# Two parts of the transposed activations in one 512-column product

## The chip, the cores and the metric

The kernel runs on one core of a Trainium2 chip, in one launch. The metric is the device time of the program in microseconds, as the median of several runs; less is better. The engines are TensorE (PE, with its weight loads as PEld), VectorE (DVE), ScalarE (ACT), GpSimd (POOL) and SyncE (SP), which here only issues transfers.

## The reference

An encoder trunk of two layers over 256 tokens of width 1024. Each layer normalises x, multiplies it with one wide input matrix, and feeds three branches: a chunkwise retention (8 heads), a sparse attention over a compressed latent, whose keys a small indexer chooses, and a cross-attention into 256 memory tokens. The branches are projected, gated with sigmoids, summed, projected once more and added to x. Then comes the feed-forward part, which is more than half of the weights that are read:

```python
        x = x + merged @ w_out[l]
        h2 = rmsnorm(x, norm2[l])
        x = x + jnp.square(jax.nn.relu(h2 @ w_ff1[l])) @ w_ff2[l]
```

All inputs and the output are float32.

## The kernel before

**Products in two parts.** Every large product is made of float32r operands. An operand a is split into a high part (a copy into float32r) and a low part (what is left), and `mm3` (L217) issues three products into one accumulation: high x high, low x high and high x low. In the code hi and lo are the parts of a weight block, xh and xl those of the activations.

**The weight stream.** All weights come as blocks of 128 x 1024 in the order of `plan()`. `load_next` has SP fetch a block into wst (four buffers); `split_next` (L154) makes whi on ACT (L162) and wlo on DVE (L163), five buffers each. `use` (L173) hands out the next block after `ahead` (L167) has issued the splits of the blocks up to four further on; the split of a block waits for the products that still read its buffer. The order of each engine's instructions is that of the program text.

**A-form and B-form.** `gemm_a` (L222) keeps the activations as stationary operand and streams 512 columns of weights past them: out rows are tokens. `gemm_b` (L234) does the reverse: a weight block of 128 output columns is stationary and the 256 tokens stream past, so the result comes out transposed. B-form serves mq (the queries of the memory attention, 4 blocks a layer), mk (the keys of the memory, 4 blocks a layer) and f1 (the first feed-forward matrix, 32 blocks a layer). Two blocks make a group: they fill one PSUM tile of 128 x (2 x 256), which `evac` then reads.

**The feed-forward part** (`ff`, L833). The first four f1 blocks are held together (ws, pp, `first`, L851), while the second half of the normalised x is still being transposed (`turn`, L860) and row statistics are made; `ahead` (L875, L878) issues splits between them; `spread` (L305) brings the row factor R into the columns' layout over a PSUM tile and an ACT copy (L310). Then `evac` (L838) makes relu, scale and square of each group: DVE (L840), ACT (L842), DVE (L843, L845). From i = 2 to 15 a step is one group of f1 followed by the products of f2 for group i - 2 (`second`, L884), A-form with the squares uh and ul as stationary operand.

**Layer 1's start.** `Between` (L905) and `k_evac` (L947): the last products of layer 0's feed-forward, `norm_half(0)`, then mk with `norm_half(1)` (L277; transposes into two PSUM tiles) between its two groups, since x's second half is finished only then. The evaluation of mk is `k_part` (L753).

**Buffers.** PSUM has eight banks, four under the tag mm and four under sd; a tile takes a whole bank. A tile gets the buffer of its tag that was released first. In SBUF the tag a4 has 22 buffers of 4 KB per partition, among them the parts of x and of the memory (`ht_pair`, L262: two buffers), and b2 has 10 of 2 KB. Attention work runs as lanes: generators that `tick` (L184) advances by a step after each weight block, with pauses counted in blocks.

```python
            for j in range(2):
                hi, lo = (v3(w, 8, 128) for w in use(name))
                for k in range(8):
                    xh, xl = xT[k // 4]
                    mm3(p[:, j], hi[:, k], lo[:, k], xh[:, k % 4], xl[:, k % 4], k == 0, k == 7)
```

Of the kernel before, what the change touches and what calls it, by code (L numbers as in the profile page):

```python
# [18 lines left out]
COLS = {"rq": 0, "rk": 512, "rv": 1024, "rg": 1536, "dsa": 2048, "mq": 2472, "g0": 2984, "g1": 4008, "g2": 5032}  # L19


# blocks of the weight stream that go by before the next step of a lane, in each layer
PAUSE = {
# [11 lines left out]
def plan():  # L35
    seq = []

    def a_form(name, l, src, c0, n, nk):
        for k in range(0, nk, 2):
            seq.append((name, src, l, "A", c0, n, k))  # L40

    def b_form(name, l, src, c0, n):
        for c in range(0, n, 128):
            seq.append((name, src, l, "B", c0 + c, 128, 0))

    def heads(l):
        a_form("dsa", l, "w_in", COLS["dsa"], 424, 8)
        for n in ("rq", "rk", "rv"):
            a_form(n, l, "w_in", COLS[n], 512, 8)
        a_form("iq", l, "w_iq", 0, 256, 2)  # L50
        b_form("mq", l, "w_in", COLS["mq"], 512)
        a_form("uq", l, "w_uq", 0, 512, 2)
        seq.append(("ukv", "w_uk", l, "K", 0, 512, 0))

    for l in range(L):
        if l:
            b_form("mk", l, "w_mem_kv", 0, 512)
        heads(l)
        a_form("rg", l, "w_in", COLS["rg"], 512, 8)
        if not l:  # L60
            b_form("mk", l, "w_mem_kv", 0, 512)
        a_form("mv", l, "w_mem_kv", 512, 512, 8)
        for b, o in ((0, "w_ret_o"), (2, "w_mem_o"), (1, "w_dsa_o")):
            for c in range(2):
                a_form(f"g{b}", l, "w_in", COLS[f"g{b}"] + 512 * c, 512, 8)
            for c in range(2):
                a_form(f"o{b}", l, o, 512 * c, 512, 4)
        for c in range(2):
            a_form("wo", l, "w_out", 512 * c, 512, 8)
        for i in range(18):  # L70
            if i < 16:
                b_form("f1", l, "w_ff1", 256 * i, 256)
            if i >= 2:
                for k in range(2):
                    seq.append(("f2", "w_ff2", l, "F", 0, 1024, 2 * (i - 2) + k))
    return seq
# [19 lines left out]
def trunk(ctx: ExitStack, tc: tile.TileContext, x, xt, mem, memt, wts, gains, rel_bias, final_norm,  # L96
# [8 lines left out]
    dr = ctx.enter_context(tc.tile_pool(name="dr", bufs=1, space=bass.MemoryType.DRAM))  # L105
    ctx.enter_context(tc.manual_schedule())

    NB = {"a4": 22, "b2": 10, "s1": 6, "st": 4, "w": 5}

    def a4(shape, name, dt=F32):  # L110
        return act.tile(shape, dt, name=name, tag="a4", bufs=NB["a4"])
# [25 lines left out]
    def bc(col, *shape):  # L137
        return col.unsqueeze(2).to_broadcast([128, *shape])

    # the weight stream: blocks arrive in the order of plan(), each split into two float32r parts  # L140
    SEQ = plan()
    OFF = np.concatenate([[0], np.cumsum([128 * block_cols(b) for b in SEQ])]).tolist()
    st_tiles, split_tiles = {}, {}
# [33 lines left out]
        pos["use"] = i + 1  # L177
        return split_tiles.pop(i)

    # attention and other work beside the products of the stream, a step after every block  # L180
    lanes = []
    now = [0]

# [38 lines left out]
    def gemm_a(name, xT, nk, n, pst):  # L222
        for k0 in range(0, nk, 2):
            hi, lo = (v3(w, 2, n) for w in use(name))
            for t in range(2):
                for j in range(2):
                    k = k0 + j
                    xh, xl = xT[k // 4]
                    mm3(pst[t][:, :n], xh[:, k % 4, tsl(t)], xl[:, k % 4, tsl(t)], hi[:, j], lo[:, j],
                        k == 0, k == nk - 1)  # L230
            if k0 < nk - 2:
                tick()

    def gemm_b(name, xT, ncols, evac):  # L234
        for c in range(0, ncols, 256):
            p = mm().rearrange("p (j t) -> p j t", j=2)
            for j in range(2):
                hi, lo = (v3(w, 8, 128) for w in use(name))
                for k in range(8):
                    xh, xl = xT[k // 4]  # L240
                    mm3(p[:, j], hi[:, k], lo[:, k], xh[:, k % 4], xl[:, k % 4], k == 0, k == 7)
                if j == 0:
                    tick()
            evac(c // 128, p)
            tick()

    def transpose4(p, src):
# [14 lines left out]
    def ht_pair(name):  # L262
        return a4([128, 4, 256], name + "h", F32R), a4([128, 4, 256], name + "l", F32R)

    def mem_load(c):
        tmp = a4([128, 4, 256], "gxt")
        nc.sync.dma_start(tmp, memt[:, 4 * c:4 * c + 4])
        return tmp

    def mem_gain(tmp, l, c):  # L270
        pair = ht_pair("gx")
        V.tensor_mul(tmp, tmp, bc(gn[:, 16 + 8 * l + 4 * c:20 + 8 * l + 4 * c], 4, 256))
        mT.append(pair)
        yield
        split_to(tmp, *pair)

    def norm_half(c, gcol):  # L277
        pair = ht_pair("xT")
        for t in range(2):
            p4 = transpose4(mm(), X[t][c])  # L280
            tmp = b2([128, 4, 128], "ntmp")
            V.tensor_mul(tmp, p4, bc(gn[:, gcol + 4 * c:gcol + 4 * c + 4], 4, 128))
            split_to(tmp, pair[0][:, :, tsl(t)], pair[1][:, :, tsl(t)])
        return pair
# [17 lines left out]
        yield  # L302
        row_rstd(X, "n1", r=rstd)

    def spread(r, name):  # L305
        p = mm()
        for t in range(2):
            PE.transpose(p[:, tsl(t)], r[:, t:t + 1].to_broadcast([128, 128]), ident)
        R = s1([128, 256], name)
        S.activation(R, p[:, :256], AF.Copy)  # L310
        return R

    # constants and inputs
    gn = cst.tile([128, 54], F32, name="gn")
    nc.sync.dma_start(gn, gains)
    zero = cst.tile([128, 512], mybir.dt.bfloat16, name="zero")
# [3 lines left out]
        PE.matmul(warm, zero[:, :128], zero, start=True, stop=True)  # L320
    xT0 = []
    for c in range(2):
        pair = ht_pair("gx")
        xT0.append(pair)
        tmp = a4([128, 4, 256], "gxt")
        for k in (0, 2):
            nc.sync.dma_start(tmp[:, k:k + 2], xt[:, 4 * c + k:4 * c + k + 2])
            load_next()
            (G if c + k else V).tensor_mul(tmp[:, k:k + 2], tmp[:, k:k + 2], bc(gn[:, 4 * c + k:4 * c + k + 2], 2, 256))
            split_to(tmp[:, k:k + 2], pair[0][:, k:k + 2], pair[1][:, k:k + 2])  # L330
            split_next()
# [501 lines left out]
    def ff(l, xT, side, tail):  # L833
        gcol = 32 + 8 * l
        us = {}
        R = []

        def evac(i, p):  # L838
            r = b2([128, 2, 256], "fr")
            V.scalar_tensor_tensor(r, p, 0.0, R[0][:, None, :].to_broadcast([128, 2, 256]), op0=OP.max, op1=OP.mult)  # L840
            uh = b2([128, 2, 256], "uh", F32R)
            S.activation(uh, r, AF.Square)  # L842
            V.tensor_mul(r, r, r)  # L843
            ul = b2([128, 2, 256], "ul", F32R)
            V.tensor_sub(ul, r, f(uh))  # L845
            us[i] = (uh, ul)

        ws = [[v3(w, 8, 128) for w in use("f1", n)] for n in range(4)]
        pp = [v3(mm(), 2, 256) for _ in range(2)]

        def first(i, kh, j):  # L851
            hi, lo = ws[2 * i + j]
            for k in range(4 * kh, 4 * kh + 4):
                xh, xl = xT[kh]
                mm3(pp[i][:, j], hi[:, k], lo[:, k], xh[:, k % 4], xl[:, k % 4], k == 0 and j == 0, k == 7,
                    skip_group_check=True)

        pair, tmps = ht_pair("xT"), []

        def turn(t):  # L860
            tmp = b2([128, 4, 128], "ntmp")
            V.tensor_mul(tmp, transpose4(mm(), X[t][1]), bc(gn[:, gcol + 4:gcol + 8], 4, 128))
            split_to(tmp, pair[0][:, :, tsl(t)], pair[1][:, :, tsl(t)])

        first(0, 0, 0)
        turn(0)
        first(0, 0, 1)
        turn(1)
        xT.append(pair)
        for j in range(2):  # L870
            first(1, 0, j)
        rstd = row_rstd(X, "n2")
        for j in range(2):
            first(0, 1, j)
        ahead(pos["use"] - 2)  # L875
        for j in range(2):
            first(1, 1, j)
        ahead(pos["use"])  # L878
        R.append(spread(rstd, "R"))
        evac(0, pp[0])  # L880
        evac(1, pp[1])
        acc = [[sd(), sd()], [sd(), sd()]]

        def second(i, k, hi, lo, c, t):  # L884
            uh, ul = us[i]
            mm3(acc[t][c], uh[:, k, tsl(t)], ul[:, k, tsl(t)], hi[:, c], lo[:, c], i == 0 and k == 0, i == 15 and k == 1)

        for i in range(2, 16):
            gemm_b("f1", xT, 256, lambda c, p: evac(i, p))
            for k in range(2):  # L890
                hi, lo = (v3(w, 2, 512) for w in use("f2"))
                for c in range(2):
                    for t in range(2):
                        second(i - 2, k, hi, lo, c, t)
                tick()
            if i in side:
                side[i]()
        last = [(i, k, *[v3(w, 2, 512) for w in use("f2", 2 * (i - 14) + k)]) for i in (14, 15) for k in range(2)]
        for c, t in tail.order:
            for i, k, hi, lo in last:  # L900
                second(i, k, hi, lo, c, t)
            V.tensor_add(X[t][c], acc[t][c], X[t][c])
            tail(c, t)
# [166 lines left out]
```

## Time and profile before

| | us |
|---|---|
| median of 3 runs | 887.86 |
| lowest and highest | 887.8 and 888.34 |
| span of the profiled execution, first to last instruction | 886.7 |
| TensorE busy in it | 876.5 |
| VectorE busy | 625.2 |
| ScalarE busy | 468.0 |

The profile is of one execution; of its own time only the span is known. Matmuls are pipelined and their ends in the profile are modelled, so the busy time of a group of products overstates what each adds; the distance from one start to the next does not. A wait is put down to the instruction whose semaphore came last.

### The profile page before, as it was taken

What the parts mean: (1) busy time and instruction counts of PE and PEld (TensorE: products, weight loads), DVE (VectorE), ACT (ScalarE), POOL (GpSimd) and SP (SyncE); (2) the same over time, 40 slices, a digit from 0 to 9 for tenths busy, and PEclk for the clock granted to TensorE, in tenths of its full rate; (3) what the DMA queues carried; (4) which work ended last, traced back from release to release, by engine and by line L of the source; (5) the groups of instructions that cost most, each with busy time, mean ns of one, the idle gap of its engine ahead of it and who ended that gap; (6) DMA issues with size and microseconds to landing.
All of it is one profiled execution on the core that took longest, in us unless ns stands there. A gap on an engine that the chain in (4) does not pass through costs nothing.

```text
span 886.7 us, 13129 instructions
## 1 busy us (share of the span) xinstructions
PE 876.5 (99%) x5119; PEld 767.1 (87%) x5119; DVE 625.2 (71%) x910; ACT 468.0 (53%) x673; POOL 21.7 (2%) x27
## 2 busy tenths in 40 slices
PE   8999999999999999999999999999999999999996
PEld 6888988888889999999898888888888999999995
DVE  5878788786777656666578758996858685555554
ACT  6576458575545444444256555676574544444442
POOL 2000110000000000000001001000000000000000
PEclk9999999999999999999999999999999999999999
DMA  8883345536354655665546543454545465666541
GB/s 310 291 304 126 118 167 170 209 120 200 134 194 137 217 186 182 203 210 190 162 153 225 179 157 98 163 189 145 176 157 174 162 211 190 190 190 190 182 152 48
DMA packets 45711, 158.76 MB, mean 179 GB/s; under 512 B 5160, under 2 KB 6480, under 8 KB 45520
## 3 DMA queue, kind: packets, MB, share of 16 engines
q1 hardware_dynamic: 45360, 157.40, 53.7%
q8 instruction: 40, 0.66, 0.3%
q10 hardware_dynamic: 288, 0.52, 0.2%
q14 instruction: 23, 0.19, 0.1%
HBM read 156.84 MB, written 1.06 MB: 178 GB/s over the span
## 4 chain that ended last, share of the span: by engine, by line
PE 98%; issue 1%; DVE 0%; DMA 0%; ACT 0%; POOLq 0%; POOL 0%; SPq 0%; DVEq 0%
PE mm L218 22%; PE mm L220 21%; PE mm L219 21%; PE sd L220 9%; PE sd L218 9%; PE sd L219 9%; PE mm L249 1%; PE sd L567 1%; PE sd L655 1%; PE sd L249 1%; PE sd L596 1%; PE sd L520 1%; PE sd L640 0%; PE sd L624 0%; PE sd L497 0%
## 5 line engine op out<-in xcount | busy, mean ns | idle before, releaser
L163 DVE TENSOR_TENSOR wlo<-wst,whi 128x1024 fp32r<-128x1024 f32 (+1 forms) x286 | 342.7, 1216 | 144.9 <-ACT whi L162 143.5
L162 ACT ACTIVATE whi<-wst 128x1024 fp32r<-128x1024 f32 (+1 forms) x286 | 297.1, 1050 | 181.6 <-PE mm L220 56.4
L218 PE MATMUL mm<-xTh,whi 128*128 128x256 f32 x544 | 154.4, 284 | 0.0
L220 PE MATMUL mm<-xTl,whi 128*128 128x256 f32 x544 | 153.8, 283 | 0.0
L219 PE MATMUL mm<-xTh,wlo 128*128 128x256 f32 x544 | 153.7, 283 | 0.0
L219 PEld LDWEIGHTS mm<-xTh,wlo 128*128 128x128 f32 x544 | 104.1, 191 | 1.3
L218 PEld LDWEIGHTS mm<-xTh,whi 128*128 128x128 f32 x544 | 104.0, 191 | 1.2
L220 PEld LDWEIGHTS mm<-xTl,whi 128*128 128x128 f32 x544 | 104.1, 191 | 0.0
L220 PE MATMUL sd<-wlo,uh 128*128 128x512 f32 x256 | 101.1, 395 | 0.0
L218 PE MATMUL sd<-whi,uh 128*128 128x512 f32 x256 | 101.0, 395 | 0.0
L219 PE MATMUL sd<-whi,ul 128*128 128x512 f32 x256 | 100.9, 394 | 0.0
L218 PE MATMUL mm<-whi,gxh 128*128 128x512 f32 (+1 forms) x208 | 82.0, 394 | 1.2 <-ACT whi L162 1.2
L220 PE MATMUL mm<-wlo,gxh 128*128 128x512 f32 (+1 forms) x208 | 81.3, 391 | 1.1 <-DVE wlo L163 1.1
L219 PE MATMUL mm<-whi,gxl 128*128 128x512 f32 (+1 forms) x208 | 81.2, 390 | 0.0
L218 PE MATMUL mm<-whi,xTh 128*128 128x512 f32 (+1 forms) x176 | 68.8, 391 | 0.0
L220 PE MATMUL mm<-wlo,xTh 128*128 128x512 f32 (+1 forms) x176 | 68.1, 387 | 0.0
L219 PE MATMUL mm<-whi,xTl 128*128 128x512 f32 (+1 forms) x176 | 68.1, 387 | 0.0
L842 ACT ACTIVATE uh<-fr 128x512 fp32r<-128x512 f32 x32 | 20.2, 632 | 77.1 <-DVE fr L840 77.1
L220 PEld LDWEIGHTS sd<-wlo,uh 128*128 128x128 f32 x256 | 48.2, 188 | 11.2
L218 PEld LDWEIGHTS sd<-whi,uh 128*128 128x128 f32 x256 | 48.4, 189 | 10.0
L219 PEld LDWEIGHTS sd<-whi,ul 128*128 128x128 f32 x256 | 48.3, 188 | 10.0
L218 PEld LDWEIGHTS mm<-whi,gxh 128*128 128x128 f32 x208 | 39.6, 191 | 9.6 <-ACT whi L162 1.8
(243 smaller groups left out, 1358.3 us busy)
## 6 DMA issues: line engine op xcount, KB each, us to landing
wst<-in_wts_dram SPq DMA_DIRECT2D x276, 512.0 KB, 3.9
wst<-in_wts_dram SPq DMA_DIRECT2D x8, 424.0 KB, 4.5
gxt<-in_memt_dram SPq DMA_DIRECT2D x4, 512.0 KB, 5.7
gxt<-in_xt_dram SPq DMA_DIRECT2D x4, 256.0 KB, 5.4
X<-in_x_dram SPq DMA_DIRECT2D x4, 256.0 KB, 5.8
decay<-in_decay_dram SPq DMA_DIRECT2D x1, 1024.0 KB, 5.4
mrow<-in_mem_dram SPq DMA_DIRECT2D x2, 512.0 KB, 5.4
Bt<-scr SPq DMA_DIRECT2D x1, 1024.0 KB, 6.9
```

What stands on the lines that cost most here:

```text
L162: S.activation(hi[:, :n], st[:, :n], AF.Copy)
L163: V.tensor_sub(lo[:, :n], st[:, :n], f(hi[:, :n]))
L218: PE.matmul(p, ah, bh, start=start, stop=False, **kw)
L219: PE.matmul(p, al, bh, start=False, stop=False, **kw)
L220: PE.matmul(p, ah, bl, start=False, stop=stop, **kw)
L249: PE.transpose(p[:, tsl(j)], src[:, tsl(j)], ident)
L520: PE.matmul(p[:, j], Q3[t][:, h + j], K3[:96], start=True, stop=True)
L567: PE.matmul(p[:, j * K:j * K + K], qd[rows, h // 2, tsl(t)], kd[rows, h // 2, :K], start=True, stop=True)
L596: PE.transpose(p[:, tsl(j)], bm[:, h0 + j - g0, tsl(s)], ident)
L655: PE.matmul(p[:, hs], sc0[h // 4][:, h % 4, tsl(t)], v[:, 0, hs], start=True, stop=t == 0)
L842: S.activation(uh, r, AF.Square)
```

## The change

The two parts of the transposed activations come to lie in one tile of a new tag, x8 (`ht_both`, four buffers of 8 KB), and a4 goes from 22 to 15 buffers. In B-form `mm2` takes the place of `mm3`: the stationary high weights meet both parts in one product of 512 columns (two runs of 256), and the low weights meet the high part in a second product of 256 columns, added to the first half. A weight block now fills a whole PSUM bank, so a group has two of them. `halves` adds the two halves at eviction: ACT copies the second half of each bank to a b2 tile, DVE adds the first half to it. The evaluations read that tile in place of PSUM. In `ff` the four held blocks take four mm banks; the transposes of `turn` and `spread` move to sd banks. `gemm_a` reads the same parts as before. The pauses of the lanes stay as they were.

```diff
@@ -105,7 +105,7 @@
     dr = ctx.enter_context(tc.tile_pool(name="dr", bufs=1, space=bass.MemoryType.DRAM))
     ctx.enter_context(tc.manual_schedule())
 
-    NB = {"a4": 22, "b2": 10, "s1": 6, "st": 4, "w": 5}
+    NB = {"a4": 15, "x8": 4, "b2": 10, "s1": 6, "st": 4, "w": 5}
 
     def a4(shape, name, dt=F32):
         return act.tile(shape, dt, name=name, tag="a4", bufs=NB["a4"])
@@ -225,23 +225,37 @@
             for t in range(2):
                 for j in range(2):
                     k = k0 + j
-                    xh, xl = xT[k // 4]
+                    xh, xl = xT[k // 4][:2]
                     mm3(pst[t][:, :n], xh[:, k % 4, tsl(t)], xl[:, k % 4, tsl(t)], hi[:, j], lo[:, j],
                         k == 0, k == nk - 1)
             if k0 < nk - 2:
                 tick()
 
+    def mm2(p, hi, lo, pair, k, start, stop):
+
+        xh, _, both = pair
+        PE.matmul(p, hi, both[:, :, k], start=start, stop=False, skip_group_check=True)
+        PE.matmul(p[:, 0], lo, xh[:, k], start=False, stop=stop, skip_group_check=True)
+
+    def halves(s, ps2):
+        for j, p in enumerate(ps2):
+            S.activation(s[:, j], p[:, 1], AF.Copy)
+            V.tensor_add(s[:, j], p[:, 0], s[:, j])
+
     def gemm_b(name, xT, ncols, evac):
         for c in range(0, ncols, 256):
-            p = mm().rearrange("p (j t) -> p j t", j=2)
+            ps2 = []
             for j in range(2):
                 hi, lo = (v3(w, 8, 128) for w in use(name))
+                p = v3(mm(), 2, 256)
+                ps2.append(p)
                 for k in range(8):
-                    xh, xl = xT[k // 4]
-                    mm3(p[:, j], hi[:, k], lo[:, k], xh[:, k % 4], xl[:, k % 4], k == 0, k == 7)
+                    mm2(p, hi[:, k], lo[:, k], xT[k // 4], k % 4, k == 0, k == 7)
                 if j == 0:
                     tick()
-            evac(c // 128, p)
+            s = b2([128, 2, 256], "bs")
+            halves(s, ps2)
+            evac(c // 128, s)
             tick()
 
     def transpose4(p, src):
@@ -262,20 +276,24 @@
     def ht_pair(name):
         return a4([128, 4, 256], name + "h", F32R), a4([128, 4, 256], name + "l", F32R)
 
+    def ht_both(name):
+        t = act.tile([128, 2, 4, 256], F32R, name=name, tag="x8", bufs=NB["x8"])
+        return t[:, 0], t[:, 1], t
+
     def mem_load(c):
         tmp = a4([128, 4, 256], "gxt")
         nc.sync.dma_start(tmp, memt[:, 4 * c:4 * c + 4])
         return tmp
 
     def mem_gain(tmp, l, c):
-        pair = ht_pair("gx")
+        pair = ht_both("gx")
         V.tensor_mul(tmp, tmp, bc(gn[:, 16 + 8 * l + 4 * c:20 + 8 * l + 4 * c], 4, 256))
         mT.append(pair)
         yield
-        split_to(tmp, *pair)
+        split_to(tmp, *pair[:2])
 
     def norm_half(c, gcol):
-        pair = ht_pair("xT")
+        pair = ht_both("xT")
         for t in range(2):
             p4 = transpose4(mm(), X[t][c])
             tmp = b2([128, 4, 128], "ntmp")
@@ -302,15 +320,14 @@
         yield
         row_rstd(X, "n1", r=rstd)
 
-    def spread(r, name):
-        p = mm()
+    def spread(r, name, p):
         for t in range(2):
             PE.transpose(p[:, tsl(t)], r[:, t:t + 1].to_broadcast([128, 128]), ident)
...
@@ -320,7 +337,7 @@
         PE.matmul(warm, zero[:, :128], zero, start=True, stop=True)
     xT0 = []
     for c in range(2):
-        pair = ht_pair("gx")
+        pair = ht_both("gx")
         xT0.append(pair)
         tmp = a4([128, 4, 256], "gxt")
         for k in (0, 2):
@@ -846,20 +863,18 @@
             us[i] = (uh, ul)
 
         ws = [[v3(w, 8, 128) for w in use("f1", n)] for n in range(4)]
-        pp = [v3(mm(), 2, 256) for _ in range(2)]
+        pp = [[v3(mm(), 2, 256) for _ in range(2)] for _ in range(2)]
 
         def first(i, kh, j):
             hi, lo = ws[2 * i + j]
             for k in range(4 * kh, 4 * kh + 4):
-                xh, xl = xT[kh]
-                mm3(pp[i][:, j], hi[:, k], lo[:, k], xh[:, k % 4], xl[:, k % 4], k == 0 and j == 0, k == 7,
-                    skip_group_check=True)
-
-        pair, tmps = ht_pair("xT"), []
+                mm2(pp[i][j], hi[:, k], lo[:, k], xT[kh], k % 4, k == 0, k == 7)
+
+        pair = ht_both("xT")
 
         def turn(t):
             tmp = b2([128, 4, 128], "ntmp")
-            V.tensor_mul(tmp, transpose4(mm(), X[t][1]), bc(gn[:, gcol + 4:gcol + 8], 4, 128))
+            V.tensor_mul(tmp, transpose4(sd(), X[t][1]), bc(gn[:, gcol + 4:gcol + 8], 4, 128))
             split_to(tmp, pair[0][:, :, tsl(t)], pair[1][:, :, tsl(t)])
 
         first(0, 0, 0)
@@ -876,9 +891,11 @@
         for j in range(2):
             first(1, 1, j)
         ahead(pos["use"])
-        R.append(spread(rstd, "R"))
-        evac(0, pp[0])
-        evac(1, pp[1])
+        R.append(spread(rstd, "R", sd()))
+        for i in range(2):
+            s = b2([128, 2, 256], "bs")
+            halves(s, pp[i])
+            evac(i, s)
         acc = [[sd(), sd()], [sd(), sd()]]
 
         def second(i, k, hi, lo, c, t):
```

## Rows read from the trace of the kernel before

**Rows 1.** Page: its head and its line of engines (busy us, share, instructions)

```profile
span 886.7 us, 13129 instructions
...
PE 876.5 (99%) x5119; PEld 767.1 (87%) x5119; DVE 625.2 (71%) x910; ACT 468.0 (53%) x673; POOL 21.7 (2%) x27
```

**Rows 2.** Waits of PE: who waited for whom, us in total, times, longest

```profile
PE mm L320 <- DVE zero L317: 1.2, 1, 1.2
PE mm L218 <- ACT whi L162: 1.2, 1, 1.2
PE mm L220 <- DVE wlo L163: 1.1, 1, 1.1
```

**Rows 3.** One feed-forward stage by window: busy us of each engine, granted clock, DMA

```profile
282.00:436.00 154.00, 154.00 (x967) 139.02 (x966) 100.15 (x103) 67.24 (x72) 0.00 (x0) 1.00 0.60 194
```

**Rows 4.** Groups by form: the short products, count | busy us, mean ns

```profile
L218 PE MATMUL mm<-xTh,whi 128*128 128x256 f32 x544 | 154.4, 284 | 0.0
...
L218 PE MATMUL mm<-gxh,whi 128*128 128x256 f32 x96 | 27.5, 286 | 0.0
```

**Rows 5.** Timeline of PE, feed-forward 0: start us, us, engine, line, operation, tiles

```profile
303.16 0.39 PE L218 MATMUL sd<-whi,uh 128*128 128x512 f32 x1
...
308.73 0.28 PE L218 MATMUL mm<-xTh,whi 128*128 128x256 f32 x1
...
314.49 0.39 PE L218 MATMUL sd<-whi,uh 128*128 128x512 f32 x1
```

**Rows 6.** Timeline of PE, an A-form stretch of layer 1: its ends

```profile
487.31 0.40 PE L219 MATMUL mm<-whi,xTl 128*128 128x512 f32 x1
...
498.01 0.38 PE L249 MATMUL sd<-ident,ra 128*128 128x128 f32 x2
```

**Rows 7.** Lines L310 and L473: durations in ns, min/median/max

```profile
L310 ACT ACTIVATE R<-mm x2: 363/365/367, 275.8 to 711.0; 128x256 f32<-128x256 f32 x2
...
L473 DVE TENSOR_TENSOR q<-mm,q x4: 418/422/426, 58.9 to 505.8; 128x256 fp32r<-128x256 f32 x4
```

**Rows 8.** Timelines of PE, ACT and DVE, start of layer 0's feed-forward

```profile
274.68 0.36 PE L218 MATMUL mm<-xTh,whi 128*128 128x256 f32 x1
...
274.79 1.06 ACT L162 ACTIVATE whi<-wst 128x1024 fp32r<-128x1024 f32 x1 [0.37 <-PE mm L220]
275.76 0.36 ACT L310 ACTIVATE R<-mm 128x256 f32<-128x256 f32 x1
...
275.89 1.23 DVE L163 TENSOR_TENSOR wlo<-wst,whi 128x1024 fp32r<-128x1024 f32 x1 [0.21 <-ACT whi L162]
277.03 0.68 DVE L840 SCALAR_TENSOR_TENSOR fr<-mm,R 128x512 f32<-128x512 f32 x1
```

**Rows 9.** Timelines of PE and DVE, start of layer 1's feed-forward

```profile
709.96 0.36 PE L218 MATMUL mm<-xTh,whi 128*128 128x256 f32 x1
...
712.30 0.68 DVE L840 SCALAR_TENSOR_TENSOR fr<-mm,R 128x512 f32<-128x512 f32 x1
```

**Rows 10.** Timelines of PE, ACT and DVE, layer 1's mk between its two groups

```profile
452.00 0.36 PE L218 MATMUL mm<-gxh,whi 128*128 128x256 f32 x1
...
451.60 0.91 ACT L162 ACTIVATE whi<-wst 128x848 fp32r<-128x848 f32 x1 [2.12 <-DMA wst<-in_wts_dram]
...
452.55 1.04 DVE L163 TENSOR_TENSOR wlo<-wst,whi 128x848 fp32r<-128x848 f32 x1 [1.03 <-ACT whi L162]
453.50 0.69 DVE L755 TENSOR_TENSOR kmt<-mm,Rm 128x512 f32<-128x512 f32 x1
```

**Rows 11.** Timelines of DVE and PE, layer 0, around the bias

```profile
179.38 1.22 DVE L556 SCALAR_TENSOR_TENSOR bm<-wk,Bt 128x1024 f32<-128x1024 f32 x1
...
181.15 0.28 PE L219 MATMUL sd<-pmT0h,vml 128*128 128x256 f32 x1
```

**Rows 12.** Windows at the start: busy us of each engine, granted clock, DMA

```profile
5.30:8.70 3.40, 1.18 (x5) 0.33 (x3) 2.60 (x4) 2.38 (x4) 1.19 (x1) 1.00 0.97 289
8.80:12.20 3.40, 3.40 (x10) 3.20 (x11) 1.81 (x3) 1.40 (x3) 2.23 (x2) 0.50 1.03 413
```

## The prediction, made before the changed kernel ran

> **What bounds the kernel now.** I read the page's head first: TensorE is busy for 876.5 of 886.7 us, VectorE for 71% and ScalarE for 53% of it [rows 1]. A busy TensorE can still be one that waits, so the list of waits comes next: in the whole execution TensorE waits three times, 3.5 us in all, for its first weights [rows 2]. The window over most of a feed-forward stage says the same from the other side: 154 us of TensorE in 154 us, beside 100 of VectorE and 67 of ScalarE [rows 3]. So TensorE's own issue rate sets the time, and any time taken out of its products comes off the end, unless the change makes it wait. There is no slack into which a new wait could fall: each one is paid in full.
>
> **What the products cost.** By shape, the products that change are those with 256 moving columns of activations: 544 + 96 triples [rows 4] (layers x (4 + 4 + 32) weight blocks x 8 = 640). The durations in these rows include a modelled end, so I take the distance between starts instead. In one feed-forward step 48 short products go from 308.73 to 314.49: 120.0 ns each [rows 5]. The 24 long ones before them (512 columns) go from 303.16 to 308.73: 232 ns each [rows 5]. In an A-form stretch 47 long ones go from 487.31 to 498.01: 227.7 ns [rows 6]. So 256 more columns cost 107.7 ns, and each product has a fixed part of some 12 ns. That fixed part is the whole gain on offer: the columns stay 768 per triple (512 + 256 for 3 x 256), and one product and one weight load of three go.
>
> **The saving.** No row has a long product whose moving operand is two runs of 256. At the A-form price a pair costs 227.7 + 120.0 = 347.7 ns for 360.0: 12.3 ns x 640 = 7.9 us. At the price of the second feed-forward product it is 352.1: 5.1 us. Far ends: if the short product's fixed part vanished behind the long one, 335.4 ns a pair, 15.7 us; if a run costs what a product costs, nothing. I take 7.9, because the A-form uses the same two kinds of tile with the roles exchanged, and the dearer product takes its weights from another pool. The Trainium skill (TensorE: Matmul & The Clock Gate, "Back-to-back issue gap") gives a fixed part of about 2.5 ns beyond the columns at full clock; by it the saving would be 2.5 x 640 = 1.6 us. The trace shows 12 here, and the sum goes by the trace.
>
> **What the eviction adds.** Per 256 output rows of weights two copies on ScalarE and two additions on VectorE of 128x256 from PSUM: 160 of each. The nearest rows are 365 ns (copy of R) and 422 ns (subtraction with a PSUM operand) [rows 7]: 58 us on ScalarE and 68 us on VectorE, which would then be at some 60% and 78% of the span. In the steady feed-forward loop that is 0.7 and 0.8 us per step of 11.3 us [rows 5], on engines with 35% or more to spare [rows 3]. Queued behind the copy, which waits for the second product block, are the square and the next weight splits, which come about 1 us later; they are up to five blocks of about 2.8 us ahead of their use [rows 5], so I charge nothing there. If that cover were gone, it would be up to 1 us in each of 28 steps.
>
> **New waits for PSUM.** Here the change is dear. A group now takes two of the four mm banks. In the steady loop the group before last has long freed its two, and at mq and layer 0's mk the banks come from work evicted well before. Two places differ.
>
> (1) At the start of each feed-forward, pp takes all four banks. The step i = 2 needs one, and the first comes free only after its addition. Program order puts that addition behind two weight splits and, for the copy, behind R. In layer 0 TensorE goes on with i = 2 at 274.68 today; the last of the two splits has ScalarE from 274.79 and VectorE from 275.89, and VectorE's next instruction starts at 277.03 [rows 8]. The addition then ends at 277.45, and with some 0.05 us of hand-over TensorE starts at 277.5: 2.8 us late. Layer 1 has the same shape (709.96 against 712.30) [rows 9]. Together 5.6 us. Behind the addition on VectorE stand the evaluation of step 0 and its square; their reader is second(0), 5.5 us after the restart, which is enough. Bounds: 0, if a bank were free; 6.6, if the addition took as long as a 512-column one.
>
> (2) At layer 1's mk, norm_half(1) takes two banks between the two groups, so group 1 needs a bank of group 0. VectorE gets to those additions only after the split whose ScalarE half starts at 451.60, late because its weights land late; VectorE is through at 453.50 [rows 10]. Addition to 453.92, TensorE at 453.97 for 452.00 today [rows 10]: 2.0 us, and 0.2 us of the saving in group 0 goes into the same wait. Bounds 0 and 2.4. What follows (dsa, two blocks of slack of about 2 us) I charge nothing.
>
> The moved transposes in ff take sd banks that out_proj has freed: nothing. The buffers: x8 takes the x and memory tiles out of a4, and 15 remain where 14 were free of them before the memory tiles' release and 18 after. Followed through the trace, one first write comes ahead of its buffer: the bias of layer 0 at 179.38, while the products on pmT0h run until about 181.4 [rows 11]. VectorE then waits 2 us; behind it are weight splits with five blocks in hand, so it costs nothing here, at most 2 us. SyncE's queue keeps its order.
>
> **Sum.** -7.9 + 5.6 + 2.0 + 0.2 = -0.1 us. The profiled execution spans 886.7; the median of 887.86 is 1.1 above that, taken as constant. 0.1 more goes because the two second splits wait for whi, whose last reader is now one short product earlier in a block (0.12 us in each layer). Forecast **887.6 us**: the gain is real and is paid back. Measurement can tell about 0.2%, 1.8 us.
>
> **Rivals.**
> - *Faster: a wait is shorter.* If the bank's addition does not stand behind the last split, each wait at (1) halves: 887.6 - 2.8 = 884.8. Against it: rows 8 show ScalarE's R directly behind that split. Chance 0.20. That no wait appears at all (879.8), or that the saving is 15.7 us (879.8): 0.07.
> - *Slower: the clock falls in the waits.* At the start TensorE pauses 1.2 and 1.1 us, works 1.18 us of 3.40, and then runs at a granted clock of 0.50, the 1.2 GHz level, for 3.4 us [rows 2, 12]. A pause of 2.8 us in one piece is longer than both together. Such a stretch passes half its columns, 1.7 us lost. In two of the three pauses that is 3.4: 891.0. It decides as soon as the granted clock after a pause is under 1. For it: the length; against it: before that fall the engine had been at work for only a few us, here for hundreds. Chance 0.20.
> - *Slower: the change does not do what it says.* If the second run of a long product is started like a product of its own, nothing is saved: 887.6 + 7.9 = 895.5. Nothing in the trace has such an operand. Chance 0.10.
> - *Slower: the fixed part is not the instruction's.* If most of the 12.3 ns goes with the columns and only a fifth (my choice) with the instruction, 640 x 2.5 ns or 1.6 us is saved and the time is 893.9. The prices of rows 5 and 6, where twice the columns cost 1.9 times and not twice, speak against it. Chance 0.05. The rule of the Trainium skill named above (same page and section) leads to this case.
>
> **How the numbers follow.** The forecast has 0.38 and lies in the band of no difference; its own range is 885.8 to 889.6. Faster has 0.20 + 0.07 = 0.27, slower 0.20 + 0.10 + 0.05 = 0.35. The range of 883.0 to 893.0 takes in the shorter waits, the saving of 5.1 (890.4), and clock falls with either saving; it leaves out the cases without waits and those without a saving.
>
> **What would show it.** Right: TensorE has 640 products fewer; in the feed-forward loop a pair takes 348 ns and a step of 11.3 us becomes 11.1; the waits of TensorE list two of about 2.8 us for the addition in halves and one of about 2 us at layer 1's mk, and none in between. Wrong: a pair at 360 ns or under 340; no TensorE wait for halves, or many small ones within the loop, which would mean that the eviction has become the bound there; a granted clock under 1 after 270 us.

## The result and the profile after

The changed kernel takes **893.95 us** (892.48 to 895.36), the one before 887.84 beside it: ratio 1.0064, 95% interval 1.005 to 1.0078. It is 0.6% slower, clear of the noise, where 887.6 was forecast, and lies 0.95 us above the range. The profiled execution took 892.48 us, with a span of 890.7. Two of the four executions lie at 892.5 with a mean granted clock of 0.995, two at 895.3 with 0.991; how far that is explained is said below.

The page of after, its head and its line of engines, answers to [rows 1]:

```profile
span 890.7 us, 12015 instructions
...
PE 873.5 (98%) x4479; PEld 734.0 (82%) x4479; DVE 654.5 (73%) x990; ACT 489.9 (55%) x753; POOL 21.8 (2%) x27
```

Read busy time and idle time apart. TensorE has 640 products fewer and is busy for 3.0 us less. It is idle for 890.7 - 873.5 = 17.2 us, where it was 10.2: 7.0 us more. So the change saved something and paid more than twice that in idle time. The list of waits of TensorE (who for whom, us in total, times, longest) has a new first line beside those of [rows 2]:

```profile
PE mm L237 <- DVE bs L243: 7.2, 3, 2.5
PE mm L337 <- DVE zero L334: 1.2, 1, 1.2
PE mm L220 <- DVE wlo L163: 1.1, 1, 1.1
PE mm L218 <- ACT whi L162: 0.9, 1, 0.9
```

Three waits for the addition that frees a PSUM bank (L243, in halves). The first stands at the start of layer 0's feed-forward; the timelines of PE, ACT and DVE there answer to [rows 8]:

```profile
273.27 0.38 PE L325 MATMUL sd<-ident,n 128*128 128x128 f32 x2
276.20 0.47 PE L237 MATMUL mm<-xT,whi 128*128 128x512 f32 x1 [2.55 <-DVE bs L243]
...
273.40 1.06 ACT L162 ACTIVATE whi<-wst 128x1024 fp32r<-128x1024 f32 x1 [0.35 <-PE mm L237]
274.37 0.37 ACT L327 ACTIVATE R<-sd 128x256 f32<-128x256 f32 x1
274.63 0.65 ACT L242 ACTIVATE bs<-mm 128x256 f32<-128x256 f32 x2
...
274.49 1.23 DVE L163 TENSOR_TENSOR wlo<-wst,whi 128x1024 fp32r<-128x1024 f32 x1 [0.18 <-ACT whi L162]
275.63 0.75 DVE L243 TENSOR_TENSOR bs<-mm,bs 128x256 f32<-128x256 f32 x2
```

This is the queue that was forecast: split, R and copy on ScalarE, split and additions on VectorE, and TensorE's next product behind them. From the last product before it to the restart, start to start, are 2.82 us, where 0.12 is usual: 2.70 more. Layer 1's feed-forward has 2.69, and layer 1's mk 2.26, with late weights ahead of the addition as in [rows 10]:

```profile
451.67 0.91 ACT L162 ACTIVATE whi<-wst 128x848 fp32r<-128x848 f32 x1 [2.33 <-DMA wst<-in_wts_dram]
...
452.62 1.04 DVE L163 TENSOR_TENSOR wlo<-wst,whi 128x848 fp32r<-128x848 f32 x1 [1.24 <-ACT whi L162]
453.57 0.75 DVE L243 TENSOR_TENSOR bs<-mm,bs 128x256 f32<-128x256 f32 x2
...
454.04 0.50 PE L237 MATMUL mm<-gx,whi 128*128 128x512 f32 x1 [2.10 <-DVE bs L243]
```

Together 7.65 us. Behind the one at mk the windows (busy us of each engine, then granted clock, DMA share, GB/s) show something that the trace before has, while TensorE has products to do, only in its first microseconds [rows 12]:

```profile
447.00:455.55 8.55, 6.45 (x40) 5.45 (x39) 6.78 (x9) 4.27 (x7) 0.00 (x0) 1.00 0.71 229
455.56:458.97 3.41, 3.41 (x13) 2.93 (x12) 2.52 (x4) 0.79 (x2) 0.00 (x0) 0.50 0.34 117
458.97:470.00 11.03, 11.03 (x60) 10.49 (x60) 7.78 (x15) 8.86 (x18) 1.09 (x2) 1.00 0.48 152
```

For 3.41 us the granted clock is 0.50, the 1.2 GHz level: 1.7 us lost, and counted as busy time. So the 3.0 us less of busy time are 1.7 lost and 4.7 saved: 7.3 ns for each of 640 pairs, where 12.3 were forecast. The loop itself, in the window of [rows 3] and in the timeline of one step as in [rows 5]:

```profile
282.00:436.00 154.00, 154.00 (x766) 129.19 (x765) 110.62 (x132) 75.23 (x100) 0.00 (x0) 1.00 0.58 192
```

```profile
304.34 0.39 PE L218 MATMUL sd<-whi,uh 128*128 128x512 f32 x1
...
309.90 0.39 PE L237 MATMUL mm<-xT,whi 128*128 128x512 f32 x1
...
315.55 0.39 PE L218 MATMUL sd<-whi,uh 128*128 128x512 f32 x1
```

TensorE never waits in it. Read as distances between these starts, the 24 products of the second feed-forward product take 5.56 us as before, the 16 pairs 5.65 us: 353.1 ns each.

### The profile page after: what moved, and what is told of

It reads as the page before. It is cut to its first block, busy times and chain, and to the rows that moved or that the text cites. A ratio compares the mean times of both kernels' runs of the same rounds, so it can differ in the third digit from the quotient of the medians.

```text
span 890.7 us, 12015 instructions
## 1 busy us (share of the span) xinstructions
PE 873.5 (98%) x4479; PEld 734.0 (82%) x4479; DVE 654.5 (73%) x990; ACT 489.9 (55%) x753; POOL 21.8 (2%) x27
## 4 chain that ended last, share of the span: by engine, by line
PE 96%; DVE 1%; issue 1%; ACT 1%; DMA 1%; POOLq 0%; POOL 0%; SPq 0%; ACTq 0%; DVEq 0%
PE mm L237 17%; PE mm L218 13%; PE mm L220 13%; PE mm L219 13%; PE sd L218 8%; PE sd L219 8%; PE sd L220 8%; PE mm L238 8%; PE sd L263 1%; PE sd L584 1%; PE sd L672 1%; DVE wlo L163 1%; PE sd L613 1%; PE mm L263 1%; PE sd L537 1%
## 5 line engine op out<-in xcount | busy, mean ns | idle before, releaser
L237 PE MATMUL mm<-xT,whi 128*128 128x512 f32 x544 | 193.8, 399 | 5.1 <-DVE bs L243 5.1
L238 PE MATMUL mm<-xT,wlo 128*128 128x256 f32 x544 | 152.6, 281 | 0.0
L237 PEld LDWEIGHTS mm<-xT,whi 128*128 128x128 f32 x544 | 102.2, 188 | 30.1 <-issue 5.5
L238 PEld LDWEIGHTS mm<-xT,wlo 128*128 128x128 f32 x544 | 102.7, 189 | 1.1
L218 PE MATMUL mm<-whi,gx 128*128 128x512 f32 (+1 forms) x208 | 82.0, 394 | 0.9 <-ACT whi L162 0.9
L220 PE MATMUL mm<-wlo,gx 128*128 128x512 f32 (+1 forms) x208 | 81.4, 391 | 1.1 <-DVE wlo L163 1.1
L219 PE MATMUL mm<-whi,gx 128*128 128x512 f32 (+1 forms) x208 | 81.2, 390 | 0.0
L218 PE MATMUL mm<-whi,xT 128*128 128x512 f32 (+1 forms) x176 | 68.7, 391 | 0.0
L219 PE MATMUL mm<-whi,xT 128*128 128x512 f32 (+1 forms) x176 | 68.1, 387 | 0.0
L220 PE MATMUL mm<-wlo,xT 128*128 128x512 f32 (+1 forms) x176 | 68.1, 387 | 0.0
L218 PEld LDWEIGHTS mm<-whi,gx 128*128 128x128 f32 x208 | 39.6, 190 | 9.2 <-ACT whi L162 1.4
L220 PEld LDWEIGHTS mm<-wlo,gx 128*128 128x128 f32 x208 | 39.5, 190 | 9.1 <-DVE wlo L163 1.4
L219 PEld LDWEIGHTS mm<-whi,gx 128*128 128x128 f32 x208 | 39.6, 190 | 7.0
```

Source lines behind the costliest of these rows:

```text
L218: PE.matmul(p, ah, bh, start=start, stop=False, **kw)
L219: PE.matmul(p, al, bh, start=False, stop=False, **kw)
L220: PE.matmul(p, ah, bl, start=False, stop=stop, **kw)
L237: PE.matmul(p, hi, both[:, :, k], start=start, stop=False, skip_group_check=True)
L238: PE.matmul(p[:, 0], lo, xh[:, k], start=False, stop=stop, skip_group_check=True)
```

## The experiments

Two questions: what the three waits cost and whether the low clock belongs to them; and why a pair costs 353 ns and not 347.7. All kernels are edits of the changed one, or of each other as said; ratios are to the kernel before (888.2 to 888.4 us on the chip of these runs).

### The waits and the clock

**e1_early** moves the additions of the first pair of banks ahead of the weight splits, at the start of both feed-forwards.

```diff
+        s0 = b2([128, 2, 256], "bs")
+        halves(s0, pp[0])
         ahead(pos["use"] - 2)
...
-        for i in range(2):
-            s = b2([128, 2, 256], "bs")
-            halves(s, pp[i])
-            evac(i, s)
+        evac(0, s0)
+        s = b2([128, 2, 256], "bs")
+        halves(s, pp[1])
+        evac(1, s)
```

> Theory (the lost time is three waits of TensorE for a PSUM bank and the clock falls after them): with group 0 evicted before the last splits, the two waits of 2.7 us at the feed-forward starts go, and with them the falls that follow them; the wait of 2.3 us at layer 1's mk and its fall stay. 892.5 - 5.4 = 887.1 us, and 1.4 us less in runs in which no fall follows the mk wait. Rival (the added eviction work or the weight stream is what is late, and the bank is only where it shows): another wait takes the place of these, time stays within 1 us of 892.5 to 895.4.

Measured: 886.6 us, ratio 0.9978 [0.9968, 0.9987]. One of the three waits is left, the one at mk:

```profile
PE mm L237 <- DVE bs L243: 1.9, 1, 1.9
```

**e2_sd** lets layer 1's norm_half(1) transpose into the sd banks, so that mk's second group finds a bank free.

```diff
-    def norm_half(c, gcol):
+    def norm_half(c, gcol, bank=mm):
...
-            p4 = transpose4(mm(), X[t][c])
+            p4 = transpose4(bank(), X[t][c])
...
-                    xT.append(norm_half(1, 8 * l))
+                    xT.append(norm_half(1, 8 * l, sd))
```

> Theory: norm_half(1) in sd banks leaves mk's second group two free mm banks, so the 2.3 us wait at layer 1's mk goes, and the fall that follows it; the two waits at the feed-forward starts stay with what falls follow them. 892.5 - 2.3 - 1.4 = 888.8 us without a fall, 891.6 with two. Rival (the late weights of the block behind mk set the end there, not the bank): the wait moves to a weight split of the next blocks, time as after, 892.5 to 895.4.

Measured: 891.77 us, 1.0035 [1.0025, 1.0046]. The wait at mk is gone from its list; the two of 2.6 us are left:

```profile
PE mm L237 <- DVE bs L243: 5.1, 2, 2.6
```

In its profiled execution the clock fell behind both of these, at places where it had held in the profiled execution of after. The windows around the first:

```profile
270.00:277.70 7.70, 5.15 (x30) 4.32 (x29) 6.26 (x7) 4.78 (x8) 0.56 (x1) 1.00 0.58 179
277.70:281.30 3.60, 3.60 (x15) 3.07 (x14) 2.74 (x5) 1.21 (x4) 0.00 (x0) 0.55 0.51 199
281.30:290.00 8.70, 8.70 (x43) 7.27 (x43) 7.45 (x10) 5.18 (x8) 0.00 (x0) 0.99 0.18 61
```

**e3_both** has both edits.

> Theory: none of the three waits and no fall after the start is left; what remains is the saving of some 4.3 us in the products: 883.5 us, every run within 0.3 us of the others. Rival (the eviction's work costs elsewhere): between 886 and 890.

Measured: 883.6 us, 0.9941 [0.9926, 0.9956]. Its waits of TensorE are all within the first 14 us:

```profile
PE mm L220 <- DVE wlo L163: 1.5, 2, 1.1
PE mm L337 <- DVE zero L334: 1.2, 1, 1.2
PE mm L218 <- ACT whi L162: 0.6, 1, 0.6
```

**e8_fill** leaves the waits as they are and gives TensorE something to do in them.

```diff
+    def fill(n):
+        p = sd()
+        for _ in range(n):
+            PE.matmul(p, zero[:, :128], zero, start=True, stop=True)
...
         R.append(spread(rstd, "R", sd()))
+        fill(12)
...
                     xT.append(norm_half(1, 8 * l))
+                    fill(9)
```

> The changed kernel with 12, 9 and 12 products of zeros set into the three waits, in a bank that nobody reads; the waits stay as long as they are. Theory (the clock falls because TensorE is idle in the waits): the granted clock stays at 1.00 from 13 us on, and all runs lie at 892.5 - 1.4 = 891.1 us. Rival (the falls and the spread of the runs have another cause): runs spread from 892.5 to 895.4 as before, with clocks of 0.995 and 0.991.

Measured: 890.81 us, 1.003 [1.0021, 1.004]. The granted clock stays at 1.00 through all three places, as in these windows of it:

```profile
445.00:470.00 25.00, 24.87 (x135) 21.59 (x135) 18.51 (x28) 15.98 (x28) 1.10 (x2) 1.00 0.52 161
270.00:285.00 15.00, 14.95 (x79) 11.66 (x79) 12.46 (x18) 7.70 (x14) 0.40 (x1) 1.00 0.41 140
710.00:720.00 10.00, 9.95 (x54) 7.45 (x55) 8.06 (x12) 5.39 (x10) 0.00 (x0) 1.00 0.63 210
```

The first of them, filled (11 of the 12 products are in the trace):

```profile
273.80 2.54 PE L243 MATMUL sd<-zero 128*128 128x512 bf16 x11
276.29 0.47 PE L237 MATMUL mm<-xT,whi 128*128 128x512 f32 x1
```

The four add up. From after (1.0064) to e8 (1.003) is 3.0 us: the low clock alone, since the products that wait for a bank still start late. From after to e3 (0.9941) is 10.9 us: 7.65 us of waits and the same 3 us. So the low clock behind these places is a consequence of the pauses: it is gone when TensorE has products to do in them, here of zeros. It does not follow every pause: in the profiled executions of after, e1 and e2 there are six, and it fell behind three, the second of after and both of e2. One such fall, as in the profiled execution of after, goes with 892.5 us; the 0.004 of mean clock between the two levels of time times 893 us is 3.6 us, about two falls more. Where those lie is not shown: the mean takes in the start too, where the profiled executions of all these kernels ran at 0.50 for anything from 0 to 6.8 us.

### What the joining is worth

**e6_split** is e3 with the long product cut in two again, into the two halves of the bank; the eviction keeps its sum.

```diff
-        PE.matmul(p, hi, both[:, :, k], start=start, stop=False, skip_group_check=True)
+        PE.matmul(p[:, 0], hi, xh[:, k], start=start, stop=False, skip_group_check=True)
+        PE.matmul(p[:, 1], hi, xl[:, k], start=False, stop=False, skip_group_check=True)
```

> Both waits removed, the joined product cut again into two of 256 columns that go to the two halves of the bank, so that the eviction's sum stays and only the joining goes. All three theories: the pair costs 3 x 120 = 360 ns again, 640 x (360.0 - 353.1) = 4.4 us more than 883.6, so 888.0 us, which is the time of the kernel before (888.3 on the same chip): the eviction's sum costs nothing. A rival for the eviction: if the added work on ScalarE and VectorE costs TensorE time somewhere, this stands over 888.3 by that much; over 889.3 would show it.

Measured: 888.32 us, 0.9996 [0.9987, 1.0005]. So the copies and additions cost TensorE nothing that shows within 1 us, and joining alone is worth 888.32 - 883.6 = 4.7 us, the amount that the page of after gave.

### Why a pair costs 353 ns

**e5_all** is e3 with the two parts laid out in turns for each block of 128 rows, so that a long product's 512 columns are one run.

```diff
-        PE.matmul(p, hi, both[:, :, k], start=start, stop=False, skip_group_check=True)
+        PE.matmul(p, hi, both[:, k], start=start, stop=False, skip_group_check=True)
...
-        t = act.tile([128, 2, 4, 256], F32R, name=name, tag="x8", bufs=NB["x8"])
-        return t[:, 0], t[:, 1], t
+        t = act.tile([128, 4, 2, 256], F32R, name=name, tag="x8", bufs=NB["x8"])
+        return t[:, :, 0], t[:, :, 1], t
```

> Both waits removed as in the run that took 883.6 us, and the transposed halves laid out side by side for each group, so that the 512 columns of a joined product are one run of addresses. There the pair of a 512 and a 256 column product took 236.0 + 117.1 = 353.1 ns; the forecast had 347.7 (227.7 + 120.0). Theory A, reading two runs costs the missing 5.4 ns: 640 x 5.4 ns = 3.5 us come back, 880.1 us, pair 347.7. Theory B, the alternation of a long and a short product costs it: 883.6, pair 353. Theory C, neither does, a 512 column product in this loop takes what the second feed-forward product always took there (232 to 233 ns): 883.6, pair 352 to 353. A and only A expects under 881.5.

Measured: 883.73 us, 0.9949 [0.9935, 0.9964]; pair 353.4 ns. Two runs cost what one costs.

**e7_batch** is e3 with all long products of a weight block first, then its short ones.

```diff
-                for k in range(8):
-                    mm2(p, hi[:, k], lo[:, k], xT[k // 4], k % 4, k == 0, k == 7)
+                mm8(p, hi, lo, xT, range(8), True, True)
...
+    def mm8(p, hi, lo, xT, ks, start, stop):
+        for k in ks:
+            PE.matmul(p, hi[:, k], xT[k // 4][2][:, :, k % 4], start=start and k == ks[0], stop=False, skip_group_check=True)
+        for k in ks:
+            PE.matmul(p[:, 0], lo[:, k], xT[k // 4][0][:, k % 4], start=False, stop=stop and k == ks[-1], skip_group_check=True)
```

> Both waits removed, the operand in two runs as in the change, but all the 512 column products of a block first and then its 256 column ones, so that lengths no longer alternate. Theory B (alternation costs the missing 5.4 ns): 512 columns at 227.7, 256 at 120.0, 880.1 us. Theories A and C: 883.6, with 512 columns at 232 or more and 256 at 120.

Measured: 882.52 us, 0.993 [0.9914, 0.9947]; pair 231.6 + 119.0 = 350.6 ns. A half step towards 347.7: within a batch the first five to seven long products take 224 to 237 ns, mostly 228 or more, and the last 226 or 227.

**e9_batch16** lets both weight blocks of a group run their long products, then both their short ones (`hi8` and `lo8` are the two loops of `mm8`).

```diff
+            for j in range(2):
+                hi, lo = (v3(w, 8, 128) for w in use(name, j))
+                ps2.append(v3(mm(), 2, 256))
+                los.append(lo)
+                hi8(ps2[j], hi, xT, range(8), True)
+            for j in range(2):
+                lo8(ps2[j], los[j], xT, range(8), True)
```

> As the run with the 512 column products of a block first (882.5 us; 231.6 + 119.0 = 350.6 ns a pair; within a batch of eight the first seven 512 column products took 229 to 236 ns and the last 226 to 227), but both blocks of a column group together: sixteen of 512 columns, then sixteen of 256. Theory: after each change of length some eight products run irregularly and long, then they settle. So the second eight should take 226 to 227, the mean 229, the 256 column ones 119.5, the pair 348.5; over the 544 pairs that run in such groups 544 x 2.1 ns = 1.1 us less, 881.4 us. Rival: what is long in this loop has nothing to do with the changes of length; then the second eight take 229 to 236 like the first, the pair stays at 350.6 and the time at 882.5, or more where the later release of the lower weights makes TensorE wait.

Measured: 882.13 us, 0.9927 [0.9911, 0.9944]; pair 230.1 + 119.6 = 349.7 ns. Its timeline of PE, one step (24 long products of the second feed-forward product, 16 long of the first, 16 short):

```profile
325.08 0.39 PE L218 MATMUL sd<-whi,uh 128*128 128x512 f32 x1
...
330.66 0.40 PE L236 MATMUL mm<-xT,whi 128*128 128x512 f32 x1
...
334.32 0.40 PE L240 MATMUL mm<-xT,wlo 128*128 128x256 f32 x2
...
336.23 0.39 PE L218 MATMUL sd<-whi,uh 128*128 128x512 f32 x1
```

232.5, 228.8 and 119.4 ns a product. In the middle group the distances between starts are 236, 224, 231, 236, 228, 233, 231 and then 226 or 227 nine times: what the theory wanted of the second eight. But the 24 before them never settle, though no length changes there: 228 to 233, with a 240 or 241 every seventh time.

**e10_stat** asks whether that is their stationary operand. It is e7 with the second product's stationary operand taken from the transposed rows; the second feed-forward product then leaves out the squared activations and the output is another function; shapes and instructions stay as they were.

```diff
-            uh, ul = us[i]
+            uh, ul = pair[:2]
```

> As the run with the 512 column products of a block first, but the second feed-forward product takes its stationary operand from the transposed normalised rows in place of the squared activations (the output is then another function; the instructions and their shapes are the same). It separates why these 512 column products take 232 to 233 ns, with 241 every few products, where the query and key products of the same shape settle at 226 to 227. If the place of the stationary operand decides, they go to 227, the step of 24 products from 5.58 to 5.45 us, and the whole by 768 x 5 ns = 3.8 us. If not, they stay at 232 and the time at 882.5 us.

Measured in a single execution: 877.36 us. The 24 now go 233, 236, 228, 233, 230 and then 226 or 227: a mean of 227.8 ns for 233.0. So the buffer matters, or that its contents had only just been written.

What sets that buffer apart in the built program is its address. Buffers follow each other in a partition in the order of their first use; the ring of ten that holds the squared activations comes after a few tiny ones and begins at 196672 bytes (192576 in the kernel before), 64 past a multiple of 2048, while the weights, the transposed rows and the other buffers of 4 KB (a4) begin 1984 past one.

**e11_place** is e9 with one unused buffer of that ring taken first, which puts the ring at 102336, and **e12_before_place** is the kernel before with the same line:

```diff
+    b2([128, 2, 256], "bs")
+
     def s1(shape, name, dt=F32):
```

> As the run with sixteen and sixteen products together (882.1 us), but the ring of ten small buffers that holds the squared activations is laid out at 102336 to 122816 bytes of a partition in place of 196672 to 217152, and the other rings move up. With the stationary operand read from a buffer at 102336 to 135104, the second feed-forward product had settled at 226 to 227 ns. If the address decides: 227 to 228 here too, 768 x 4.5 ns = 3.5 us less, 878.6 us; and transposed rows that now lie above 196544 should make their own products slow. If it was not the address but that this operand has just been written, or is waited for: 232 to 233 as before, 882.1 us.

> The kernel before with that layout alone. If the address decides: 888.2 less 3.5, so 884.7 us, with the short products unchanged at 120 ns. If not: 888.2.

Measured: e11 877.73 us, 0.9878 [0.9863, 0.9892]; e12 885.21 us, 0.9966 [0.9954, 0.9979]. The second product takes 228.6 and 227.9 ns. The other half of the expectation did not come: rows that now lie at 200640 and 208832 have products of 226 to 227 ns. So it is neither the height in the partition nor that the operand is freshly written. At 102336 the ring is also 1984 past a multiple of 2048.

**e13_phase** leaves the ring at the top and puts 1920 bytes ahead of it, so that it too begins 1984 past a multiple of 2048 (e9 otherwise).

```diff
+    pad = []
+
     def b2(shape, name, dt=F32):
+        if not pad:
+            pad.append(act.tile([128, 480], F32, name="pad", tag="pad", bufs=1))
```

> As the run with sixteen and sixteen products together (882.1 us), the ring of small buffers still at the top of the partition but 1920 bytes higher, 198592 in place of 196672. All other operands of the products begin at 1984 bytes past a multiple of 2048 there, the ring at 64 past one; with the 1920 bytes it begins at 1984 too. In the run with the ring low, rows of other products lay at 200640 and 208832 and their products still took 226 to 227 ns. If the offset decides: the second feed-forward product at 227 to 229, 878 us. If the place in the partition decides: 232 to 233, 882.

Measured: 877.71 us, 0.988 [0.9862, 0.9899]. Its timeline of PE for the step that e9 was shown for:

```profile
325.30 0.40 PE L222 MATMUL sd<-whi,uh 128*128 128x512 f32 x1
...
330.77 0.39 PE L240 MATMUL mm<-xT,whi 128*128 128x512 f32 x1
...
334.40 0.28 PE L244 MATMUL mm<-xT,wlo 128*128 128x256 f32 x1
...
336.31 0.40 PE L222 MATMUL sd<-whi,uh 128*128 128x512 f32 x1
```

227.9, 226.9 and 119.4 ns: the step takes 11.01 us for 11.15. The 1920 bytes move this ring and the small buffers above it, none of which feeds these products, so the offset decides, at either place. And the long products of the first kind, which follow the second product without a change of length, no longer begin irregularly: what was irregular had been carried over.

**e14_alt_place** is e3, with its alternation, and the ring low as in e11.

> Both waits removed (883.6 us) and the ring of small buffers laid out low, with long and short products still alternating as in the change. If the alternation by itself costs the missing 5.4 ns of a pair: the pair stays at 353, and only the second feed-forward product gets shorter, 768 x 4.5 ns = 3.5 us, 880.1 us. If the irregular products of the step before carry over into the pairs, the pair falls to 348 to 350 and the time to 877 to 878.

Measured: 881.51 us, 0.9918 [0.9901, 0.9934]; pair 236.6 + 116.9 = 353.5 ns, second product 228.3. The alternation costs its 5.3 ns (against the 348.2 of e13) by itself, behind regular products too; why it does is not shown. The time fell by 2.1 us, of the 768 x (232.7 - 228.3) ns = 3.4 us that these distances give; the difference lies within the two intervals, each about 1.4 us to either side.

All of it side by side, with the mean distances between starts in ns (over the 544 pairs on xT, that is without the 96 of the memory keys; over the second feed-forward product):

| kernel | long + short | pair | second product | us |
|---|---|---|---|---|
| before | three of 120.2 | 360.7 | 232.4 | 887.84 |
| after | 236.5 + 117.1 | 353.6 | 232.0 | 893.95 |
| e3, waits gone | 236.0 + 117.1 | 353.1 | 232.7 | 883.6 |
| e6, and cut again | three of 120.2 | 360.6 | 232.5 | 888.32 |
| e5, e3 in one run | 236.1 + 117.3 | 353.4 | 232.6 | 883.73 |
| e14, e3 and offset | 236.6 + 116.9 | 353.5 | 228.3 | 881.51 |
| e7, eights | 231.6 + 119.0 | 350.6 | 233.0 | 882.52 |
| e9, sixteens | 230.1 + 119.6 | 349.7 | 233.0 | 882.13 |
| e11, e9 and ring low | 228.6 + 119.6 | 348.2 | 228.6 | 877.73 |
| e13, e9 and offset | 228.6 + 119.6 | 348.2 | 228.6 | 877.71 |

e11 and e13 take 1.2% less than the kernel before.

## Why the prediction was wrong, step by step

- **What bounds the kernel** was right: each wait of TensorE was paid in full, and each ns of its products came off the end (e6 against e3).
- **The saving is the step that failed.** "At the A-form price a pair costs 227.7 + 120.0" took two prices from stretches in which neighbours have one length. Between short products the long one takes 236 ns and the short one 117. The saving is 4.7 us for 7.9, a mis-sized term of 3.2 us, and less than the 5.1 that stood as the other price. The reason given against that other price, that "the dearer product takes its weights from another pool", had hit on the cause of its 232 ns without knowing it: the operand's place. It only did not help the pair (e14). With neighbours of one length and the offset mended, a pair takes 346.3 ns in the step shown of e13, and 348.2 over all its pairs: there the forecast price holds.
- **The Trainium skill's** 2.5 ns (TensorE: Matmul & The Clock Gate, "Back-to-back issue gap") does not fit these float32r products either: dropping one product of three gives 7.5 ns in the alternation (e6 to e3) and 13.7 without it (360.0 to 346.3). It does fit the filling products of e8, which are bfloat16: they follow at 216 ns for 512 columns. The rival that this rule led to had 893.9 us, next to the measured time, but by chance: it had a saving of 1.6 us and no low clock.
- **Two runs of the moving operand** cost nothing beyond one (e5): that rival falls.
- **The eviction** was right in what it costs: no wait in the loop, and nothing in e6. By step it was about right too: VectorE and ScalarE are busy for 110.62 and 75.23 us in the window where [rows 3] had 100.15 and 67.24, some 0.8 and 0.6 us a step. Its count over the whole was twice too high. Each of the 80 weight blocks gives one copy and one addition, so there are 80 of each and not 160 (990 instructions on VectorE for 910, 753 on ScalarE for 673), and the engines came to 73% and 55% of the span, not 78% and 60%. Nothing in the forecast hung on it.
- **The waits** were right in place, cause and size: 2.8, 2.8 and 2.0 forecast, 2.70, 2.69 and 2.26 measured. Nothing else waits.
- **The clock** was put at nothing in the sum and stood as a rival with a chance of 0.20; it is what happened on top. The argument against it, that TensorE had worked for hundreds of microseconds before, did not hold: the clock fell all the same, for the forecast 1.7 us each time, though not behind every pause. Nor did the length decide: in the profiled execution of after it fell behind the shortest of the three.
- **The sum** then reads: -4.7 + 7.65 = +2.95, so 890.8 us; e8, with its waits and no fall, took 2.5 us more than the kernel before (890.81 for 888.29). 3.0 us of low clock make it 893.8. The two misses, 3.2 and 3.0 us, are about equal. One small term was added up wrongly: 0.12 us in each of two layers is 0.24, not 0.1, and the forecast's own terms give 887.5. The range was too short by its own terms: the saving of 5.1 (890.4) with two falls (3.4) is 893.8, and it ended at 893.0.

## What to carry to other kernels

A product's price belongs to a sequence: take it from a stretch with the same neighbours, not from one with the same shape. A pause of TensorE of 2.4 to 2.8 us can cost its own length and 1.7 us of low clock behind it; if it cannot be removed, the clock part can be filled away with products that nobody reads. When a tile that feeds an already full PSUM pool doubles its banks, look for the places where all banks are taken at once, and evict there ahead of the next weight split: the same change was worth 0.6% with two small edits (when a bank is evicted, and which banks a transpose takes), and cost 0.6% without.

## What was not expected of the hardware

- The granted clock fell to 0.50 for 3.4 us behind pauses of 2.4 and 2.8 us (from start to start), behind one in one execution and behind others in another: behind the second of three in that of after, behind both in that of e2, and not behind the single one of 2.15 us in that of e1. No profiled execution with TensorE at work through these places showed it.
- Products that alternate between 512 and 256 columns settle into a pattern of 233, 117, 241, 120, 236, 113 ns, in which no long one takes 227; after one change of length five to seven long products are irregular (e7, e9, e13).
- A 512-column product takes 232 to 233 ns instead of 227 when its stationary operand begins 64 bytes, and not 1984, past a multiple of 2048. Only these two offsets were tried; whether the offset itself or its distance to that of the moving operand counts stays open. The kernel before loses 3.1 us to it.
